# Decoder layer on one core: block products on 12 of 24 row tiles in four down products, with partial sums kept in DRAM

## The chip, the core and the metric

The kernel runs on one core of a Trainium2 chip. Its engines work side by side, each through its own list of instructions in order: PE (matrix products, and the loads of their stationary operand, PEld), DVE (two-operand arithmetic), ACT (copies, casts, activation functions), POOL (a general engine, used here for little) and SP (issues transfers). ACT and POOL issue transfers too. An instruction waits for semaphores of the others. The metric is the time of one execution in microseconds (us) on the device, less is better; it is given as the median of several runs, and one more execution was profiled.

## What is computed

A decoder layer on 256 tokens of width 2048, all in float32: an FFN, a mixer (attention beside a recurrent group) and a second FFN, each added to its scaled input and normalised. The change lies in the two FFNs alone:

```python
def swiglu(x, w_gate, w_up, w_down):
    return (jax.nn.silu(x @ w_gate) * (x @ w_up)) @ w_down
...
        x = layer_norm(alpha * x + 0.5 * swiglu(x, ffn1_w_gate[l], ffn1_w_up[l], ffn1_w_down[l]),
                       ln1_g[l], ln1_b[l])
        p = x @ w_in[l]
...
        mix = jnp.concatenate([o_attn, o_rwkv], axis=-1) @ w_out[l]
        x = layer_norm(alpha * x + mix, ln2_g[l], ln2_b[l])
        x = layer_norm(alpha * x + 0.5 * swiglu(x, ffn2_w_gate[l], ffn2_w_up[l], ffn2_w_down[l]),
                       ln3_g[l], ln3_b[l])
```

The gate and up weights are 2048 x 5632, the down weights 5632 x 2048; alpha is the fourth root of 2.

## The kernel before

**Split operands.** Every float32 operand of a large product is cut into a high part (rounded to the matrix engine's faster float format) and a low part (the rest). A product of two tiles is three matmuls: high x high, high x low of the weight, low x high (`product`, lines 151 to 153). Activations are cut once; weights are cut on the way in: a raw tile of two row tiles (128 x 1024 elements) is loaded by SP (`load`, L131), ACT casts its high part `wh` (L141), DVE subtracts for its low part `wl` (L144). The pair (`wh`, `wl`) lies in one of seven buffer pairs, used in turn (`halves`).

**Tiling.** 256 tokens are two token tiles (t = 0, 1) of 128. Weights go by row tiles of 128 rows and column blocks of 512. A matmul has 128 x 128 activations as the stationary and 128 x 512 weights as the moving operand. The 44 column blocks of the hidden width are done in two halves: 24 row tiles (six blocks of four) and then 20. For each half, gate and up are computed block by block, the hidden activations are transposed and cut into tiles `hh` (`up_done`), and then the down product adds the half's part to the layer's 2048 outputs.

**Block products.** `two_blocks` computes two column blocks at once, for both token tiles. Of the row tiles, the first eight are taken as a 2 x 2 block matrix (two groups of four row tiles by two column blocks), and the activations likewise (two token tiles by two groups of four). Their product is done in seven block products in place of eight (Winograd's form of Strassen's method): the products use sums and differences of the raw weights (`minus`, L222, DVE, in place, 128 x 2048 elements) and of the activations (`combinations`, four sums `s` that are computed, then cut into two parts each, L379 and L383). Each of the seven is `seven(...)`: two weight pairs, 12 matmuls. Partial results move between PSUM banks by ACT copies (L235, L242, L248) and DVE additions (L251, L255). The remaining row tiles go the plain way: `later` makes a list of steps of two row tiles for one column block (one weight pair, 12 matmuls for both token tiles), and `late(n)` runs n of them between the block products. The steps of the second column block are left in the list for the next call. Raw tiles of block products are four row tiles each in four buffers (`r4`), those of plain steps two row tiles in three buffers (`raw`).

**Down products.** A half calls `two_blocks` twice, for columns 0 to 1023 and 1024 to 2047. `down_done` takes each finished 128 x 512 sum: in the first half it adds alpha times the residual (loaded into `rc` by a transfer on ACT's queue, L477, which a one-column POOL copy at L476 holds back until there is use for it) and writes into the SBUF tile `y` (L478); in the second half it adds the sum to `y` and starts the normalisation (L316 on). `y0` and `y1`, 128 x 2048 each, hold these partial sums from the first half's down products to the end of the FFN. `y0` is the scratch tile of `combinations` before.

**Order.** The program is written in the order of the code; a scheduler with a cost model then puts each engine's instructions in an order by readiness and priority, which is fixed when the program is compiled. `issue_after` adds an order by hand. A tile with a tag gets its memory when the last user of the tag's former tile is done.

## Time and profile before

| | |
|---|---|
| median of 3 runs | 1919.73 us (1919.19 to 1925.22) |
| the profiled execution, its own time | 1918.89 us |
| its span, first to last instruction | 1917.1 us |
| granted PE clock, mean | 0.996 |
| FFN1 | about 0 to 680 us; its first half's down products about 252 to 377 us |
| mixer | about 680 to 1205 us |
| FFN2 | about 1206 us to the end; its first half's down products about 1456 to 1581 us |
| moved from and to HBM | 368.29 MB read, 11.80 MB written, 198 GB/s |

How to read it: a group row has the source line, engine, operation and tiles (out<-in), its count, busy time in us and the mean ns of one instruction, and after the second bar the idle time of that engine just before them with what ended it. A row of the order in time has the start, the length in us, engine, line and operation, and in brackets the idle time before it. In a row of waits, who waited for whom is followed by the total in us, how many times, and the longest. Lines (L144) are those of the code above. Matmuls are pipelined: the 390 ns of one overlap those of the next.

### The profile page before, as it was taken

What the parts mean: (1) busy time and instruction counts of PE and PEld (TensorE: products, weight loads), DVE (VectorE), ACT (ScalarE), POOL (GpSimd) and SP (SyncE); (2) the same over time, 40 slices, a digit from 0 to 9 for tenths busy, and PEclk for the clock granted to TensorE, in tenths of its full rate; (3) what the DMA queues carried; (4) which work ended last, traced back from release to release, by engine and by line L of the source; (5) the groups of instructions that cost most, each with busy time, mean ns of one, the idle gap of its engine ahead of it and who ended that gap; (6) DMA issues with size and microseconds to landing.
All of it is one profiled execution on the core that took longest, in us unless ns stands there. A gap on an engine that the chain in (4) does not pass through costs nothing. (4 is left out here: it accounts for less than half of the span.)

```text
span 1917.1 us, 24935 instructions
## 1 busy us (share of the span) xinstructions
PE 1881.4 (98%) x9335; PEld 1547.7 (81%) x9335; DVE 1623.1 (85%) x1834; ACT 1093.9 (57%) x1376; POOL 74.9 (4%) x110
## 2 busy tenths in 40 slices
PE   8999999999999999999999999999999999999997
PEld 7888888888888878887778877788888888888886
DVE  8999987789999976776678886999999778999986
ACT  6656664566666536645565543566666545666651
POOL 0000101100000000000000000000000110000000
PEclk9999999999999999999999999999999999999999
DMA  9766676765667456555445645775566676566744
GB/s 312 246 201 217 185 239 220 233 212 200 216 213 228 143 172 201 167 159 160 139 132 146 188 135 165 257 255 191 197 214 227 208 245 211 198 205 212 223 159 134
DMA packets 207322, 381.73 MB, mean 199 GB/s; under 512 B 23531, under 2 KB 25649, under 8 KB 206945
## 3 DMA queue, kind: packets, MB, share of 16 engines
q1 hardware_dynamic: 182928, 350.53, 55.7%
q0 software_dynamic: 6832, 15.32, 3.0%
q10 hardware_dynamic: 17440, 14.29, 2.6%
q8 instruction: 73, 1.20, 0.3%
q14 instruction: 49, 0.39, 0.1%
HBM read 368.29 MB, written 11.80 MB: 198 GB/s over the span
## 5 line engine op out<-in xcount | busy, mean ns | idle before, releaser
L141 ACT CAST wh<-raw 128x1024 fp32r<-128x1024 f32 (+2 forms) x833 | 852.6, 1047 | 596.6 <-PE acc L153 365.9
L144 DVE TENSOR_TENSOR wl<-raw,wh 128x1024 fp32r<-128x1024 f32 (+2 forms) x833 | 983.3, 1213 | 207.7 <-ACT wh L141 203.7
L152 PE MATMUL acc<-wl,xh 128*128 128x512 f32 (+1 forms) x1552 | 604.6, 391 | 4.0 <-DVE wl L144 4.0
L153 PE MATMUL acc<-wh,xl 128*128 128x512 f32 (+1 forms) x1552 | 603.2, 390 | 0.5 <-DVE xl L90 0.4
L151 PE MATMUL acc<-wh,xh 128*128 128x512 f32 (+1 forms) x1552 | 597.8, 393 | 5.9 <-ACT xh L89 4.6
L151 PEld LDWEIGHTS acc<-wh,xh 128*128 128x128 f32 x1552 | 291.7, 188 | 69.3 <-ACT xh L89 6.2
L152 PEld LDWEIGHTS acc<-wl,xh 128*128 128x128 f32 x1552 | 292.0, 188 | 63.6 <-DVE wl L144 5.4
L153 PEld LDWEIGHTS acc<-wh,xl 128*128 128x128 f32 x1552 | 292.0, 188 | 61.8 <-DVE xl L90 2.0
L222 DVE TENSOR_TENSOR raw<-raw,raw 128x2048 f32<-128x2048 f32 x112 | 255.8, 2284 | 1.0 <-DMA raw<-in_ffn_w_gate_dram 0.5
L152 PE MATMUL acc<-wl,hh 128*128 128x512 f32 x544 | 212.0, 390 | 0.0
L153 PE MATMUL acc<-wh,hh 128*128 128x512 f32 x544 | 211.4, 389 | 0.0
L151 PE MATMUL acc<-wh,hh 128*128 128x512 f32 x544 | 210.9, 390 | 0.0
L151 PE MATMUL acc<-wh,s 128*128 128x512 f32 x448 | 174.9, 390 | 1.0 <-ACT acc L248 1.0
L153 PE MATMUL acc<-wh,s 128*128 128x512 f32 x448 | 174.6, 390 | 0.0
L152 PE MATMUL acc<-wl,s 128*128 128x512 f32 x448 | 174.4, 389 | 0.0
L151 PEld LDWEIGHTS acc<-wh,hh 128*128 128x128 f32 x544 | 102.1, 188 | 21.7 <-ACT wh L141 0.4
L152 PEld LDWEIGHTS acc<-wl,hh 128*128 128x128 f32 x544 | 102.2, 188 | 21.1
L153 PEld LDWEIGHTS acc<-wh,hh 128*128 128x128 f32 x544 | 102.1, 188 | 20.9
L151 PEld LDWEIGHTS acc<-wh,s 128*128 128x128 f32 x448 | 84.1, 188 | 19.0 <-ACT acc L248 1.5
L153 PEld LDWEIGHTS acc<-wh,s 128*128 128x128 f32 x448 | 84.1, 188 | 17.5
L152 PEld LDWEIGHTS acc<-wl,s 128*128 128x128 f32 x448 | 84.1, 188 | 17.4
L235 ACT COPY acc<-acc 128x512 f32<-128x512 f32 x28 | 16.0, 571 | 51.5 <-PE acc L153 47.7
(264 smaller groups left out, 1100.0 us busy)
## 6 DMA issues: line engine op xcount, KB each, us to landing
raw<-in_ffn_w_up_dram SPq DMA_DIRECT2D x176, 512.0 KB, 5.3
raw<-in_ffn_w_down_dram SPq DMA_DIRECT2D x176, 512.0 KB, 5.4
raw<-in_ffn_w_gate_dram SPq DMA_DIRECT2D x175, 512.0 KB, 4.5
raw<-in_w_in_dram SPq DMA_DIRECT2D x96, 512.0 KB, 3.7
raw<-in_w_out_dram SPq DMA_DIRECT2D x32, 512.0 KB, 4.1
sd<-s POOLq DMA_DIRECT2D x16, 256.0 KB, 4.1
s<-sd POOLq DMA_DIRECT2D x16, 256.0 KB, 5.1
xs<-y ACTq DMA_DIRECT2D x16, 256.0 KB, 3.0
```

Of the source, the lines that this page charges most:

```text
L141: SC.copy(out=wh[:, c, :w], in_=raw[:, c, :w])
L144: self.cut = V.tensor_tensor(out=wl[:, c, :w], in0=raw[:, c, :w], in1=wh[:, c, :w].bitcast(F32), op=ALU.subtract).ins
L151: T.matmul(a, hi, wh[:, j, :w], start=first and j == 0, stop=False, skip_group_check=True)
L152: T.matmul(a, hi, wl[:, j, :w], start=False, stop=False, skip_group_check=True)
L153: i = T.matmul(a, lo, wh[:, j, :w], start=False, stop=last and j == 1, skip_group_check=True)
L222: V.tensor_tensor(out=out, in0=x, in1=y, op=ALU.subtract)
L235: SC.copy(out=u, in_=a)
```

## The change

In the two down calls of each FFN's first half, `extra` is set. There the block products cover 12 row tiles, not 8: each of the seven has two row tiles more (`whole` and `comb` map j = 4, 5 to them), so three weight pairs and 18 matmuls, and the plain steps cover 12 row tiles, not 16. `own` loads a second raw tile of two row tiles for each of the four blocks, and `minus` runs on both. The activations of the third group of four row tiles (hidden block 2) get their own sums, at half width, by `half_tiles`. For room, the seventh pair's two buffers and `y0`'s place hold the additional raw tiles, so the calls use six weight pairs; `y1`'s place holds the additional activation sums. The partial sums therefore leave SBUF: `down_done` writes its result in place in `rc` and stores it to DRAM tiles `ys` on ACT's queue, and `y` is loaded back by POOL's queue in the second call of the second half (j = 1).

```diff
@@ -203,9 +203,9 @@
                 for t in range(2):
                     use(t)
 
-        def two_blocks(self, cols, ks, x, comb, done, strict=False):
+        def two_blocks(self, cols, ks, x, comb, done, strict=False, extra=None):
             assert not self.pend
-            self.buffers(NW["ffn"], LAG["ffn"])
+            self.buffers(NW["ffn"] - (extra is not None), LAG["ffn"])
             (s0, c0), (s1, c1) = cols
             if self.roles is None:
                 self.roles = [(self.rot + i) % NACC["ffn"] for i in range(6)]
@@ -215,34 +215,46 @@
             a, z, u, w = (self.bank(i) for i in self.roles[:4])
             row = ks[0][0]
 
-            def own(src, k, c):
-                return self.load(src, row + k, c, n=4)
+            done_rows = 8
+            if extra is not None:
+                done_rows = 12
+                more = dict(zip(("11", "12", "22", "21"), extra()))
+
+            def own(src, k, c, name):
+                r = [self.load(src, row + k, c, n=4)]
+                if extra is not None:
+                    t = more[name]
+                    self.loaded = nc.sync.dma_start(out=t, in_=src[(row + 8 + k // 2) * P:(row + 10 + k // 2) * P, c:c + NB].rearrange("(k p) n -> p k n", p=P)).ins
+                    r.append(t)
+                return r
 
             def minus(out, x, y):
-                V.tensor_tensor(out=out, in0=x, in1=y, op=ALU.subtract)
+                for o, a, b in zip(out, x, y):
+                    V.tensor_tensor(out=o, in0=a, in1=b, op=ALU.subtract)
 
             def seven(acc, lhs, raw, first=False, last=False):
-                for i in range(2):
-                    self.product(acc, lambda j: lhs(2 * i + j), *self.halves(raw[:, 2 * i:2 * i + 2]), first and i == 0, last and i == 1)
+                parts = [raw[0][:, 0:2], raw[0][:, 2:4]] + raw[1:]
+                for i, r in enumerate(parts):
+                    self.product(acc, lambda j: lhs(2 * i + j), *self.halves(r), first and i == 0, last and i + 1 == len(parts))
 
             def whole(t, k):
-                return lambda j: x(t, k + j)
+                return lambda j: x(t, k + j if j < 4 else 4 + k // 2 + j)
 
             n = len(self.tail) // 4
             with tc.issue_after(self.loaded) if strict else ExitStack():
-                r11 = own(s0, 0, c0)
+                r11 = own(s0, 0, c0, "11")
             seven(a, whole(0, 0), r11, True)
             SC.copy(out=u, in_=a)
             self.late(n)
             with tc.issue_after(self.loaded) if strict else ExitStack():
-                r12 = own(s1, 0, c1)
+                r12 = own(s1, 0, c1, "12")
             minus(r11, r12, r11)
             seven(z, comb(0), r11, True, True)
             s5 = self.pool.tile([P, NB], F32, tag="s5", name=nm("s5"))
             SC.copy(out=s5, in_=z)
             self.late(n)
             with tc.issue_after(self.loaded) if strict else ExitStack():
-                r22 = own(s1, 4, c1)
+                r22 = own(s1, 4, c1, "22")
             minus(r11, r22, r11)
             seven(u, comb(1), r11)
             SC.copy(out=w, in_=u)
@@ -254,9 +266,9 @@
             v = self.bank(self.roles[4])
             V.tensor_tensor(out=v, in0=w, in1=s5, op=ALU.add)
             with tc.issue_after(self.loaded) if strict else ExitStack():
-                r21 = own(s0, 4, c0)
+                r21 = own(s0, 4, c0, "21")
             seven(a, whole(0, 4), r21)
-            self.later(s0, c0, ks[8:], x, (a, w), lambda t, acc: done(0, t, acc), False)
+            self.later(s0, c0, ks[done_rows:], x, (a, w), lambda t, acc: done(0, t, acc), False)
             n = len(self.tail) // 4
             self.late(n)
             seven(u, comb(3), r22)
@@ -264,7 +276,7 @@
             minus(r11, r21, r11)
             seven(w, whole(1, 4), r11)
             self.late(len(self.tail))
-            self.later(s1, c1, ks[8:], x, (u, v), lambda t, acc: done(1, t, acc), False)
+            self.later(s1, c1, ks[done_rows:], x, (u, v), lambda t, acc: done(1, t, acc), False)
 
         def flush(self, lag=0):
             uses = []
@@ -373,13 +385,13 @@
 
         S = {}
 
-        def combinations(x, tmp, after=None):
+        def combinations(x, tmp, after=None, own=None):
             def add(out, x, y, op=ALU.add):
                 x, y = (a if a.dtype == F32 else a.bitcast(F32) for a in (x, y))
                 V.tensor_tensor(out=out, in0=x, in1=y, op=op)
 
             def cut(x, i):
-                hi, lo = s_tiles(i)
+                hi, lo = (own or s_tiles)(i)
                 SC.copy(out=hi, in_=x)
                 add(lo, x, hi, ALU.subtract)
 
@@ -403,7 +415,7 @@
             return S[i]
 
         def comb(i):
-            return lambda j: (S[i][0][:, j, :], S[i][1][:, j, :])
+            return lambda j: tuple(s[:, j, :] for s in S[i]) if j < 4 else tuple(s[:, j - 4, :] for s in S[4 + i])
 
         def y_parts():
             t = fp.tile([P, 4, 4, P], F32, tag="y0", name=nm("xs"))
@@ -411,6 +423,24 @@
 
         def x_parts():
             return [xp.tile([P, 4, P], F32, tag=f"{t}0{q}", name=nm("xs")) for q in range(2) for t in ("xh", "xl")]
+
+        def half_tiles(x):
+            u = fp.tile([P, 8, 2, P], F32R, tag="y1", name=nm("s"))
+            t = fp.tile([P, 4, 2, P], F32, tag="y0", name=nm("xs"))
+
+            def own(i):
+                S[4 + i] = [u[:, 2 * i], u[:, 2 * i + 1]]
+                return S[4 + i]
+
+            combinations({(a, q): [h[:, 2 * q:2 * q + 2] for h in x[(a, 2)]] for a in range(2) for q in range(2)},
+                         [t[:, i] for i in range(4)], None, own)
+
+        def more_raws():
+            r = [fp.tile([P, 2, NB], F32, tag=f"{n}6", name=nm("raw")) for n in ("wh", "wl")]
+            t = fp.tile([P, 4, NB], F32, tag="y0", name=nm("raw"))
+            return r + [t[:, 0:2], t[:, 2:4]]
+
+        ys = [dp.tile([P, D], F32, tag=f"ys{t}", name=nm("ys")) for t in range(2)]
 
         for half, nj in enumerate((6, 5)):
             hT = {}
@@ -457,6 +487,10 @@
                         for i in range(4):
                             for k, t in enumerate(s_tiles(i)):
                                 nc.gpsimd.dma_start(out=t, in_=sd[i, k])
+                    if half == 1 and j == 1:
+                        y.extend(fp.tile([P, D], F32, tag=f"y{t}", name=nm("y")) for t in range(2))
+                        for t in range(2):
+                            nc.gpsimd.dma_start(out=y[t], in_=ys[t])
                     stream.two_blocks(((wg, c0), (wu, c0)), KX, x_lhs, comb, lambda i, tt, acc, f=(gate_done, up): f[i](tt, acc), j0 + j == 1)
 
             def h_lhs(tt, k, hT=hT):
@@ -465,7 +499,7 @@
 
             combinations(hT, (y_parts, x_parts)[half]())
             if half == 0:
-                y.extend(fp.tile([P, D], F32, tag=f"y{t}", name=nm("y")) for t in range(2))
+                half_tiles(hT)
             if half == 0 and extra is not None:
                 extra(hT[(0, 0)][0][:, 0, 0:1].bitcast(F32))
 
@@ -475,7 +509,8 @@
                     rc = fp.tile([P, NB], F32, tag="sg", name=nm("rc"), bufs=2)
                     G.tensor_copy(out=rc[:, 0:1], in_=hT[(0, 0)][0][:, 0, 0:1].bitcast(F32))
                     nc.scalar.dma_start(out=rc, in_=res[tt][:, c])
-                    V.scalar_tensor_tensor(out=y[tt][:, c], in0=rc, scalar=ALPHA, in1=acc, op0=ALU.mult, op1=ALU.add)
+                    V.scalar_tensor_tensor(out=rc, in0=rc, scalar=ALPHA, in1=acc, op0=ALU.mult, op1=ALU.add)
+                    nc.scalar.dma_start(out=ys[tt][:, c], in_=rc)
                 else:
                     ln_stats(tt, y[tt][:, c], acc, st[tt], n)
                     if n == 3:
@@ -483,7 +518,8 @@
 
             ks = [(j0 * 4 + k, k) for k in range(nj * 4)]
             for n in (0, 2):
-                stream.two_blocks(((wd, n * NB), (wd, (n + 1) * NB)), ks, h_lhs, comb, lambda i, tt, acc, n=n, f=down_done: f(tt, acc, n + i))
+                stream.two_blocks(((wd, n * NB), (wd, (n + 1) * NB)), ks, h_lhs, comb, lambda i, tt, acc, n=n, f=down_done: f(tt, acc, n + i),
+                                  extra=more_raws if half == 0 else None)
             if half == 1:
                 gb.extend(load_gb_over_x(lg, lb))
                 stream.flush(NW["ffn"] - 1)
```

## Prediction

> **What bounds the kernel now.** I read first the page's busy times with its slices, then the chain of work that ended last, then the busy times by window around the down products of each FFN's first half (252 to 377 us in FFN1, 1456 to 1581 us in FFN2, 125 us for two calls each), and there the waits, the groups and the order in time.
>
> ```profile
> PE 1881.4 (98%) x9335; PEld 1547.7 (81%) x9335; DVE 1623.1 (85%) x1834; ACT 1093.9 (57%) x1376; POOL 74.9 (4%) x110
> PE   8999999999999999999999999999999999999997
> DVE  8999987789999976776678886999999778999986
> PE 36%; DVE 1%; issue 0%; ACT 0%; DVEq 0%
> ```
> ```profile
> 252.00:377.00 125.00, 125.00 (x558) 103.46 (x557) 100.67 (x89) 68.33 (x73) 13.73 (x16) 1.00 0.70 232
> 1456.00:1581.00 125.00, 125.00 (x557) 103.61 (x557) 99.54 (x85) 67.08 (x71) 13.09 (x16) 1.00 0.69 225
> 420.00:505.00 85.00, 85.00 (x384) 70.54 (x383) 77.91 (x66) 52.52 (x59) 0.00 (x0) 1.00 0.60 199
> ```
> The columns after the window are its length, then busy time (and instructions) of PE, weight load, DVE, ACT, POOL, then granted clock, DMA share and GB/s. PE has work in every slice and is busy for the whole of both down windows; the chain names PE and hardly anything else (the shares it can name). So time is won by taking matmuls away, as long as DVE and ACT deliver the split weights early. In gate and up (420 to 505) DVE is busy 77.91 of 85, or 92%; in the down windows 100.67 of 125, or 81%. The down products are where DVE has spare time, and that is where the change adds work.
>
> ```profile
> 239.40 0.39 PE L151 MATMUL acc<-wh,xh 128*128 128x512 f32 x1
> 252.09 0.39 PE L153 MATMUL acc<-wh,xl 128*128 128x512 f32 x1
> DVE wl L144 <- ACT wh L141: 23.4, 16, 5.2
> ACT wh L141 <- PE acc L153: 21.6, 16, 2.8
> ACT wh L141 <- DMA raw<-in_ffn_w_down_dram: 15.3, 9, 5.4
> ACT wh L141 <- POOL rc L476: 3.8, 1, 3.8
> ```
> The first two rows are the first and last of 57 matmuls in a row: 12.69 us over 56 steps is 0.227 us a matmul; the 390 ns of one overlap the next. The other four are waits in 252 to 377 (total, times, longest). DVE waits 23.4 us, nearly all for ACT's cast; ACT in turn waits most often for a matmul to free a weight pair: then all seven pairs are full and DVE is as far ahead as it can be. The waits for DMA and for POOL are of another kind: they don't shrink by themselves when DVE has more to do.
>
> **The change, part by part.** *Matmuls, removed.* A call multiplies 8 of its 24 row tiles in seven block products of 4 row tiles, 3 matmuls each (84), and 16 in the plain way, 4 x 3 each (192): 276. With 12 row tiles it is 7 x 6 x 3 = 126 and 12 x 12 = 144: 270. Six fewer a call, four calls: 24 x 0.227 = 5.44 us less on PE, which is the bound. The page "TensorE: Matmul & The Clock Gate" of the Trainium skill (Part 1) gives N ÷ 2.4 GHz plus about 2.5 ns, 215.7 ns for 512 columns, by which the saving would be 5.18 us; this trace's rows are 5% slower.
>
> *Casts and combinations of weights, added.* Pairs split per call: 7 x 2 + 16 = 30 before, 7 x 3 + 12 = 33 after. Each of the four subtractions of raw weights gets a second one of half the size.
>
> ```profile
> L144 DVE TENSOR_TENSOR wl<-raw,wh 128x1024 fp32r<-128x1024 f32 x63 | 74.6, 1219 | 23.9 <-ACT wh L141 23.4
> L222 DVE TENSOR_TENSOR raw<-raw,raw 128x2048 f32<-128x2048 f32 x9 | 20.6, 2284 | 0.0
> L141 ACT CAST wh<-raw 128x1024 fp32r<-128x1024 f32 x61 | 62.0, 1051 | 51.0 <-PE acc L153 21.6 <-DMA raw<-in_ffn_w_down_dram 15.3 <-DVE raw L222 6.2
> L952 DVE TENSOR_TENSOR BK<-BK,vv 128x1024 f32<-128x1024 f32 x2 | 2.4, 1217 | 0.0
> L947 DVE TENSOR_TENSOR BK<-BK 128x1024 f32<-128x1024 f32 x2 | 2.5, 1225 | 9.0 <-ACT BK L945 9.0
> L903 DVE TENSOR_TENSOR St<-St,PC 128x256 f32<-128x256 f32 x4 | 1.6, 411 | 0.0
> L1026 DVE SCALAR_TENSOR_TENSOR s<-s,rr 128x256 f32<-128x256 f32 x8 | 3.8, 478 | 0.0
> L799 ACT COPY BT<-sm 128x256 f32<-128x256 f32 x16 | 5.0, 380 | 7.0 <-PE sm L797 7.0
> ```
> Per FFN DVE gets 6 more splits at 1.22 us (7.3) and 8 subtractions of 128x1024 at 1.22 (1.217 to 1.225; 9.8). ACT gets 6 casts at 1.05 (6.3). *The third block of the activations*: 8 additions and 4 residues of 128x256 on DVE, 0.41 us each by the nearest tensor row (0.48 by the other), 4.9 us (to 5.7), and 4 casts on ACT at 0.38, 1.5 us. Together 22.0 us on DVE and 7.8 on ACT per FFN. The listed durations overlap their neighbours: the splits' busy time is 74.6 for 63, or 1.18 each, so about 26 x 0.04 = 1 us comes off: 21 us.
>
> DVE's stage then holds 100.7 + 21 = 121.7 us, against PE's 125 - 2.7 = 122.3. ACT holds 76 and stays cover. So nothing is left of DVE's 24 us of idle time: what hides the added work is idle time that was lost in waiting for full buffers, and the lead that DVE has.
>
> *Where it pinches.* The half-size activation block needs the scratch tile of the full-size combinations, so it can't be done early; it falls in front of the first down call, in which the first combined product needs it.
>
> ```profile
> 251.16 2.35 DVE L144 TENSOR_TENSOR wl<-raw,wh 128x1024 fp32r<-128x1024 f32 x2
> 257.91 0.39 PE L151 MATMUL acc<-wh,s 128*128 128x512 f32 x1
> 1454.08 3.49 DVE L144 TENSOR_TENSOR wl<-raw,wh 128x1024 fp32r<-128x1024 f32 x3
> 1461.70 0.39 PE L151 MATMUL acc<-wh,s 128*128 128x512 f32 x1
> 294.54 4.63 DVE L144 TENSOR_TENSOR wl<-raw,wh 128x1024 fp32r<-128x1024 f32 x4 [4.38 <-ACT wh L141]
> 314.69 2.36 DVE L144 TENSOR_TENSOR wl<-raw,wh 128x1024 fp32r<-128x1024 f32 x2 [2.04 <-ACT wh L141]
> 357.01 4.63 DVE L144 TENSOR_TENSOR wl<-raw,wh 128x1024 fp32r<-128x1024 f32 x4 [5.21 <-ACT wh L141]
> ```
> In FFN1 the first split in front of that product ends at 251.16 + 1.2 = 252.4 and PE takes it at 257.91: a lead of 5.5 us. In FFN2 it is 1461.70 - 1455.3 = 6.4 us. Put in front now: 4.9 (activation block), 1.2 (third pair of the first product), 1.2 (second subtraction), 7.3 us; PE gets 6 matmuls more to do first, 1.4 us. Short by 7.3 - 1.4 - 5.5 = 0.4 us in FFN1, covered by 0.5 us in FFN2. The next product repeats it: 3 splits, one plain split, 2.28 + 1.22 of subtraction make 8.4 us on DVE against 30 matmuls, 6.8 us: short by another 1.6. I take PE stalls of 0.4 + 1.6 = 2.0 us in FFN1 and 1.6 - 0.5 = 1.1 in FFN2. After that a call gives back: the plain steps at its end (four splits, 4.9 us, for 48 matmuls, 10.9 us) refill the buffers. Bounds: none, where the schedule spreads the block over gaps; and all 7.3 us a FFN where the lead is already spent.
>
> *Six weight pairs, not seven.* 276 matmuls for 30 pairs are 9.2 matmuls, 2.1 us, a pair: the lead shrinks by that much, but the waits of 4.4 and 5.2 us (294.54, 357.01) are still within the 12.5 us of six pairs. Nothing by itself; a rival with the rest. *Loads.* The queue of SP issues 24 weight loads of 512 KB a call, as before (8 + 16; now 8 + 4 + 12), so bytes don't change. Two of the new raw tiles take the seventh pair's place and two the old place of the partial sums, which their last users free during the call before.
>
> *Partial results through DRAM.*
> ```profile
> xs<-y ACTq DMA_DIRECT2D x16, 256.0 KB, 3.0
> lnb<-in_ln_b_dram POOLq DMA_DIRECT2D x1, 1024.0 KB, 8.3
> rc<-xs ACTq DMA_DIRECT2D x16, 256.0 KB, 5.4
> ```
> Per FFN 8 stores of 256 KB on ACT's queue (3.0 us to land, as the like store) and 2 loads of 1 MB on POOL's queue (8.3). The loads are issued in the second call of the second half, whole calls before the sums are used; POOL has nothing behind them that PE waits for. That is 4 MB a FFN; 232 GB/s take a DMA share of 70%, so the other 30% is some 100 GB/s, 40 us for 4 MB that are spread over the 125 us and the calls behind: hidden. The stores do one thing more: a store waits on ACT for the addition, and casts queue behind it. The scratch tile comes free 3 us later, so the next prefetch of the residual waits, and ACT behind it; the nearest row is the 3.8 us wait for POOL above, once in this window, which PE does not feel (2.04 us of DVE idle at 314.69). I take nothing for it; its ends are 0 and 3.8 us for each of 4 pairs of sums a FFN, 30 us if no cover were left. A gain beyond the 5.44 has no place to come from, PE having no gap in these windows.
>
> *Sum.* -5.4 + 2.0 + 1.1 = -2.3 us on the profiled execution of 1918.9 us (span 1917.1): 1916.6. The median of the runs, 1919.7, is 0.8 above it, so 1917.4. About 0.3% (5.8 us) is what a measurement of this kernel can tell from no change, and the whole saving is 0.28%.
>
> **The rivals.** *All of it is hidden.* If the stalls stay under 1 us, the saving shows whole: 1919.7 - 5.4 = 1914.3. For it: ACT waits 21.6 us for full buffers in this window, so DVE could do that much more at once. Against it: 21 us is added, at its densest where the lead is 5.5.
>
> *DVE becomes the bound.* The three long pauses quoted above (4.38, 2.04 and 5.21, 11.6 us) stay, since loads and POOL cause them, on top of 121.7 us of work: 133.3 against PE's 122.3, 11 short a FFN. If the lead of 5.5 covers half of it, 5.5 us a FFN come on top of my stalls: 1917.4 + 11 = 1928; with no cover 1917.4 + 22 = 1939. It decides from 2.7 us of stall a FFN on. For it: 92% DVE load in the calls that follow, which give the lead back slowly (7 us in 85). Against it: those waits fall where DVE had run ahead, and loads are asked for as DVE frees raw tiles, so a slower DVE meets them later. The Trainium skill's "Trace Analysis" (Identifying the Most-Contended Engine) does not count matmul busy time but that of the weight loads: here 103.46 of 125 for these, 100.67 for DVE, so by that rule DVE takes the lead as the most contended engine after the change, and the time would go this way; the trace's even spacing of 0.227 us speaks for PE so far.
>
> *A stall halves the clock.*
> ```profile
> 1206.00:1213.00 7.00, 6.29 (x20) 4.56 (x20) 7.00 (x10) 2.60 (x4) 0.00 (x0) 0.52 0.72 226
> ```
> Where PE had pauses between the mixer and FFN2, the clock fell to 0.52 for 7 us. If one stall of the down stage were as long, some 3.4 us would come on top each time: 2 stalls, 1917.4 + 2 x 3.4 = 1924. Against it: my stalls are of 1 to 2 us, and the clock is 1.00 in both windows. (The clock gate's page, Part 1, names an idle window of about 3.4 us; this rival needs one stall that long, and no run here shows the limit.)
>
> **How the numbers follow.** Partly hidden, stalls of 1 to 8 us in all: 0.47, with its own range 1915 to 1922. All hidden: 0.25. DVE as the bound, 9 us and up: 0.18. Halved clock: 0.07. Something else, mostly an order of instructions that this change upsets elsewhere: 0.03. The time is that of the first, 1917.4. From 1913.6 (all hidden, less 0.7 of scatter among runs) to 1929 leaves out less than 2 in 10. Faster by over 0.3% needs under 1914.0: a third of the all-hidden case, 0.08. Slower by over 0.3%, above 1925.5: 0.15 of the DVE case, 0.04 of the clock's and 0.02 of the rest, 0.21. Within: 0.71.
>
> **What would show it.** Right: 24 fewer matmuls; PE still full in the down windows but for two short waits near the first combined product of each FFN, for a split or a cast; DVE at 97% or more there; ACT's waits for free weight pairs gone in these stages and back in the second half's gate and up. Wrong: DVE busy clearly below that while PE waits (then it is loads or ACT's queue: look for casts waiting for POOL or for the addition); waits of PE through both calls (DVE is the bound); a clock below 1.00 there.

## The result and the profile after

| | before | changed |
|---|---|---|
| median, measured side by side | 1922.1 us (4 runs) | 1935.17 us (1933.85 to 1935.93, 4 runs) |
| ratio, 95% interval | | 1.0075 [1.0059, 1.0091] |
| profiled execution, span | 1917.1 us | 1933.8 us |
| matmuls | 9335 | 9311 |

The change makes the kernel 0.75% slower by the ratio, 13 us by the medians. 1917.4 us was forecast, and 1929.0 was the upper end.

Page of the changed kernel: busy times, and the slices of PE and of its granted clock.

```profile
PE 1884.8 (97%) x9311; PEld 1546.6 (80%) x9311; DVE 1661.3 (86%) x1886; ACT 1109.0 (57%) x1396; POOL 81.0 (4%) x114
PE   8999989999999999999999999999998999999997
PEclk9999989999999999999999999999999999999999
```

The 24 matmuls are gone, and yet PE is busy for longer: part of the matmuls ran at a lower clock. The 8 in the sixth slice of both rows (242 to 290 us) is where FFN1's down products begin.

Busy time by window of the changed kernel (columns as in the prediction): the two down stages, a stretch of gate and up, and the 11 us inside the first stage where PE loses most.

```profile
252.00:377.00 125.00, 118.78 (x508) 96.25 (x507) 107.55 (x102) 71.41 (x78) 14.90 (x14) 0.96 0.67 227
1463.00:1588.00 125.00, 117.96 (x502) 95.22 (x501) 106.61 (x97) 71.40 (x77) 14.30 (x14) 0.97 0.65 216
420.00:505.00 85.00, 85.00 (x385) 70.54 (x384) 78.16 (x66) 53.03 (x59) 0.00 (x0) 1.00 0.68 233
279.00:290.00 11.00, 7.91 (x20) 5.55 (x21) 8.82 (x10) 4.91 (x6) 1.93 (x2) 0.53 0.51 175
```

PE was busy for 125.00 of 125 in both windows before. Now it misses 6.2 and 7.0 us, and the clock is below 1.00. Gate and up are as they were. In the same 125 us PE gets through 508 matmuls in place of 558.

Order in time on PE of the changed kernel, the rows with a pause in FFN1 and in FFN2 (start, length, in brackets the pause and what ended it):

```profile
277.34 0.66 PE L459 MATMUL tr<-ident,sg 128*128 128x128 f32 x4 [1.92 <-DVE sg L456]
281.16 0.79 PE L151 MATMUL acc<-wh,s 128*128 128x512 f32 x1 [3.16 <-ACT wh L141]
284.95 0.63 PE L153 MATMUL acc<-wh,s 128*128 128x512 f32 x1
286.24 0.79 PE L151 MATMUL acc<-wh,s 128*128 128x512 f32 x1 [0.66 <-ACT acc L260]
289.88 0.40 PE L151 MATMUL acc<-wh,s 128*128 128x512 f32 x1
...
1543.57 0.73 PE L151 MATMUL acc<-wh,hh 128*128 128x512 f32 x2 [1.34 <-ACT wh L141]
1546.14 0.63 PE L153 MATMUL acc<-wh,hh 128*128 128x512 f32 x1
```

The pauses stand at block products on sums (`s`) and at the transposes beside them in the first call of FFN1 (277 to 286 us) and of FFN2, and once at a plain product (`hh`) in the second call of FFN2 (1543.57). Behind them a matmul takes 0.63 us, not 0.39: that is the halved clock. It lasts for 10.2 us from 279.2, for 3.4 us from 1494.3 and for 3.4 us from 1545.5.

A ledger over the matmuls of the two down stages (240 to 390 us and 1440 to 1600 us) adds up how far the distance from one matmul's start to the next exceeds what it is without a pause (0.227 us for two matmuls of 512 columns): before 0.4 and 0.2 us, changed 11.4 and 12.7. That is 23.5 us more lost. 5.4 us were saved by fewer matmuls, so 18 us are left. A second count gives the same: the time from one matmul ahead of a stage to one behind it, taken at the same two matmuls in both profiles, is 8.3 us longer in FFN1 and 9.7 in FFN2, 18.0 together. The spans differ by 16.7 only, because the code outside, which is the same, ran 1.0 us slower at the start and 2.4 us faster between the stages in this execution. Of the 23.5 us, 13.3 are the pauses themselves (6.2 and 7.0 in the windows above) and some 7 are matmuls at half clock (17.1 us, of which 2.9 are pauses, at half the pace); the rest was not resolved further.

What PE waited for in the first calls is DVE, mostly through ACT. Order in time on DVE of the changed kernel around FFN1's first pauses:

```profile
266.12 4.63 DVE L144 TENSOR_TENSOR wl<-raw,wh 128x1024 fp32r<-128x1024 f32 x4
270.66 0.42 DVE L391 TENSOR_TENSOR s<-xs,s 128x256 fp32r<-128x256 f32 x1
270.99 1.22 DVE L144 TENSOR_TENSOR wl<-raw,wh 128x1024 fp32r<-128x1024 f32 x1
272.13 2.29 DVE L233 TENSOR_TENSOR raw<-raw,raw 128x2048 f32<-128x2048 f32 x1
274.33 2.36 DVE L144 TENSOR_TENSOR wl<-raw,wh 128x1024 fp32r<-128x1024 f32 x2
276.60 0.69 DVE L456 SCALAR_TENSOR_TENSOR sg<-sg,acc 128x512 f32<-128x512 f32 x1
277.20 2.36 DVE L233 TENSOR_TENSOR raw<-raw,raw 128x1024 f32<-128x1024 f32 x2
279.47 0.69 DVE L456 SCALAR_TENSOR_TENSOR sg<-sg,acc 128x512 f32<-128x512 f32 x1
```

No row has a bracket: DVE runs without a break. The last step of gate and up (L456) stands behind a full-size subtraction and two splits, so PE's transposes (L459) come late. Behind it stand two of the new half-size subtractions (277.20 to 279.56), and the cast that PE waits for next starts at 280.06; ACT had stood for 1.37 us behind POOL until then. Over the whole window DVE is idle for 17 us, but not here.

DVE's work also comes to PE by a longer way, through POOL and then ACT. Rows of DVE, POOL, ACT and PE of the changed kernel in front of the longest pause of FFN2:

```profile
1488.97 3.50 DVE L144 TENSOR_TENSOR wl<-raw,wh 128x1024 fp32r<-128x1024 f32 x3
1489.30 3.33 POOL L510 COPY rc<-hh 128x1 f32<-128x1 f32 x2 [228.24 <-PE tr L459]
1492.94 0.58 ACT L469 CAST hh<-tr 128x512 fp32r<-128x512 f32 x1 [3.15 <-POOL rc L510]
1494.07 0.60 PE L151 MATMUL acc<-wh,s 128*128 128x512 f32 x1 [2.41 <-ACT acc L260]
```

POOL's one-column copies, which hold back the residual's prefetch, end just behind DVE's run of splits (1492.63 after 1492.47). ACT has the prefetch ahead of its other work and stands for 3.15 us; its copy of a partial sum (L260) starts at 1493.44, and PE has waited 2.41 us for it. So the question was: which part of the added DVE work, at which place, makes the pauses?

### The profile page after: what moved, and what is told of

Its sections match the earlier page's. It is cut to its first block, busy times and chain, and to the rows that moved or that the text cites. A ratio compares the mean times of both kernels' runs of the same rounds, so it can differ in the third digit from the quotient of the medians.

```text
span 1933.8 us, 25000 instructions
## 1 busy us (share of the span) xinstructions
PE 1884.8 (97%) x9311; PEld 1546.6 (80%) x9311; DVE 1661.3 (86%) x1886; ACT 1109.0 (57%) x1396; POOL 81.0 (4%) x114
## 5 line engine op out<-in xcount | busy, mean ns | idle before, releaser
L141 ACT CAST wh<-raw 128x1024 fp32r<-128x1024 f32 (+1 forms) x845 | 865.1, 1047 | 602.0 <-PE acc L153 394.8
L144 DVE TENSOR_TENSOR wl<-raw,wh 128x1024 fp32r<-128x1024 f32 (+1 forms) x845 | 997.5, 1216 | 189.3 <-ACT wh L141 184.3
L233 DVE TENSOR_TENSOR raw<-raw,raw 128x2048 f32<-128x2048 f32 (+1 forms) x128 | 275.5, 2155 | 1.9 <-DMA raw<-in_ffn_w_up_dram 1.1
L151 PE MATMUL acc<-wh,s 128*128 128x512 f32 x480 | 190.0, 396 | 8.9 <-ACT wh L141 4.9
L152 PE MATMUL acc<-wl,hh 128*128 128x512 f32 x504 | 197.1, 391 | 0.0
L153 PE MATMUL acc<-wh,hh 128*128 128x512 f32 x504 | 196.8, 391 | 0.0
L151 PE MATMUL acc<-wh,hh 128*128 128x512 f32 x504 | 192.7, 391 | 1.3 <-ACT wh L141 1.3
L152 PE MATMUL acc<-wl,s 128*128 128x512 f32 x480 | 188.9, 394 | 0.7 <-DVE wl L144 0.7
L153 PE MATMUL acc<-wh,s 128*128 128x512 f32 x480 | 188.6, 393 | 0.0
L151 PEld LDWEIGHTS acc<-wh,s 128*128 128x128 f32 x480 | 91.2, 190 | 31.2 <-ACT wh L141 6.9
L151 PEld LDWEIGHTS acc<-wh,hh 128*128 128x128 f32 x504 | 94.6, 188 | 21.9 <-ACT wh L141 2.5
L152 PEld LDWEIGHTS acc<-wl,hh 128*128 128x128 f32 x504 | 94.9, 188 | 19.9
L153 PEld LDWEIGHTS acc<-wh,hh 128*128 128x128 f32 x504 | 95.0, 189 | 19.7
L153 PEld LDWEIGHTS acc<-wh,s 128*128 128x128 f32 x480 | 91.2, 190 | 19.2
```

The lines of the kernel that those rows point to most:

```text
L141: SC.copy(out=wh[:, c, :w], in_=raw[:, c, :w])
L144: self.cut = V.tensor_tensor(out=wl[:, c, :w], in0=raw[:, c, :w], in1=wh[:, c, :w].bitcast(F32), op=ALU.subtract).ins
L151: T.matmul(a, hi, wh[:, j, :w], start=first and j == 0, stop=False, skip_group_check=True)
L152: T.matmul(a, hi, wl[:, j, :w], start=False, stop=False, skip_group_check=True)
L153: i = T.matmul(a, lo, wh[:, j, :w], start=False, stop=last and j == 1, skip_group_check=True)
L233: V.tensor_tensor(out=o, in0=a, in1=b, op=ALU.subtract)
```

## The experiments

All ratios are against the kernel before, measured beside it. Line numbers in rows are those of the kernel that was run.

**Partial sums through DRAM alone** (kernel before, plus this):

```diff
-V.scalar_tensor_tensor(out=y[tt][:, c], in0=rc, ...)
+V.scalar_tensor_tensor(out=rc, in0=rc, ...)
+nc.scalar.dma_start(out=ys[tt][:, c], in_=rc)
...
```

(Not shown: `y` is loaded back on POOL's queue, as in the changed kernel.)

> The kernel before with the partial sums alone sent through DRAM (12 row tiles, six pairs and the additional tiles left out; full computation). Theory A (the sums of the third activation block come late, in front of the first down call, and PE starves there): nothing here but the stores' wait on ACT, which DVE's spare time covers: within 2 us of before, no new clock drop. Theory C (a store, its landing, the POOL copy and ACT's prefetch hold up the casts): ACT still waits 7 to 8 us once per FFN, PE pauses over 1 us near the second down call, 3 to 8 us slower than before.

1922.64 us, ratio 1.0000 [0.9990, 1.0011]. Window of this kernel:

```profile
252.00:377.00 125.00, 125.00 (x557) 103.42 (x557) 99.73 (x88) 67.11 (x72) 11.14 (x15) 1.00 0.70 240
```

PE stays full. The stores and loads alone cost nothing that can be measured.

**Six weight pairs alone** (kernel before, `NW["ffn"] - 1` in the first half's down calls):

> The kernel before with six weight pairs, not seven, in the first half's down calls; nothing else. Theories A and C: no difference, under 1 us, PE without a pause there. A rival, that the shorter lead by itself starves PE: pauses in the down windows and over 3 us slower.

1922.65 us, 1.0004 [0.9992, 1.0017]. Nothing.

**Without the half-width activation sums** (changed kernel; the third row-tile group's sums are left out and slices of the full-width sums stand in their place):

```diff
-                half_tiles(hT)
+                for i in range(4):
+                    S[4 + i] = [s[:, 0:2] for s in S[i]]
```

> The changed kernel without the half-width sums of the third activation block: the additional products take slices of the sums that are there, so the output differs; 12 DVE and 4 ACT instructions fewer per FFN, and the additional raw tiles no longer wait for that scratch tile. Theory A: the pauses of PE near the first combined products (6.0 us in FFN1, 5.5 in FFN2) and the clock drops of 10.2 and 3.4 us there go; 10 to 13 us faster than the changed kernel, about 1924. Theory B (DVE is short in the whole stage, whatever the place): only the 4.5 us a FFN of this work come back, less than 7 us in all, and pauses remain. Theory C: the drop of the clock at the second down call of FFN2 stays in either case.

1932.99 us, 1.0057 [1.0040, 1.0074]. **Half-width sums ahead of the full-width ones** (changed kernel, all work done; `half_tiles(hT)` moved in front of `combinations(hT, ...)`):

> The changed kernel with the half-width sums written ahead of the full-width ones, so that they use the scratch tile first and can run in gaps of gate and up; all work is done. Theory A: like the run without these sums, about 1924, pauses at the first combined product gone or under 2 us. Theory B: no gain, within 3 us of the changed kernel, since DVE has as much to do.

1933.09 us, 1.0056 [1.0039, 1.0073]. Order in time on PE, pauses of the first (280.22) and second call of the kernel with the sums moved:

```profile
280.22 0.50 PE L151 MATMUL acc<-wh,s 128*128 128x512 f32 x1 [0.66 <-ACT acc L260]
329.12 0.50 PE L151 MATMUL acc<-wh,s 128*128 128x512 f32 x1 [1.42 <-ACT wh L141]
331.01 0.73 PE L151 MATMUL acc<-wh,hh 128*128 128x512 f32 x2 [1.39 <-ACT wh L141]
1541.80 0.73 PE L151 MATMUL acc<-wh,hh 128*128 128x512 f32 x2 [2.41 <-ACT wh L141]
1544.17 0.79 PE L151 MATMUL acc<-wh,s 128*128 128x512 f32 x1 [1.64 <-ACT wh L141]
```

The first call's pauses shrink to 0.7 us and less in FFN1 and to 1.0 us and less in FFN2, but new ones open in the second call, with a halved clock in both FFNs. My first theory, that the sums came too late and pushed one pile in front of the first call, fell: PE arrives earlier and meets the next pile. In this second pile DVE is not the last link: it stood idle itself for 1.62 us before 327.20, waiting for ACT's cast, and ACT had stood for 5.76 us with the prefetch ahead of it.

**Without the second subtractions** (changed kernel; the 16 subtractions of the additional raw tiles are left out):

```diff
-                for o, a, b in zip(out, x, y):
+                for o, a, b in list(zip(out, x, y))[:1]:
```

> The changed kernel without the second, half-width subtraction of raw weights (16 DVE instructions of 1.2 us fewer; left out, so the output differs). Theory A is dropped: the runs without the half sums and with them early gained only 2 us, and a pause near the second down call stayed. Theory B (the stage as a whole has too much DVE work in front of the combined products, so each of the two calls of a stage starves): 20 us of DVE work less, most of the pauses gone, 8 to 14 us faster than the changed kernel. Theory C (ACT held by the prefetch of the residual): the pauses at the second call stay, 2 to 5 us faster.

1916.99 us, 0.9981 [0.9971, 0.9990]. Window of this kernel:

```profile
252.00:377.00 125.00, 124.97 (x556) 103.09 (x555) 107.15 (x102) 75.58 (x82) 9.85 (x14) 1.00 0.71 240
```

PE is full, the clock 1.00, and the saving shows; ACT still waits for POOL's copies, in FFN2's window up to 4.4 us at a time, and PE has no pause from it. DVE is as busy in this window as in the changed kernel (107.15 against 107.55), since it gets through more of the call. **Without either** (both edits above, both pieces of work left out):

> The changed kernel without the half-width sums and without the second subtractions (left out, so the output differs); the three more splits a call stay, and ACT's queue is as in the changed kernel. Theory B: no pauses, the saving shows, 1914 to 1917. Theory C: the pause at the second call stays, 1919 to 1924.

1916.75 us, 0.9980 [0.9968, 0.9991]: the half-width sums cost nothing once the second subtractions are gone.

**The second subtraction on its own tile** (changed kernel; it has the same length and place but reads only the tile that it writes, so it waits for no other load; its result is another):

> The changed kernel with the second subtractions kept as DVE work of the same length in the same place, but each reading its own tile alone (it subtracts the tile from itself, so the output differs): the wait for the other block's additional raw tile is gone. Theory B (DVE time in front of the combined products): as slow as the changed kernel, 1930 to 1936. Rival D (the wait for a second raw tile, which comes late since its place is freed late): near the run without the second subtractions, 1917 to 1921.

1933.61 us, 1.0071 [1.0059, 1.0083], as slow as the changed kernel. It is DVE's time at that place, not the wait for a second tile.

**The same DVE time at the end of the call** (second subtractions left out; in each call eight 128x512 subtractions without use are put among the plain steps behind the last block product):

```diff
-            self.late(len(self.tail))
+            for i in range(len(self.tail)):
+                self.late(1)
+                for _ in range(2 if extra is not None and i < 4 else 0):
+                    V.tensor_tensor(out=s5, in0=s5, in1=s5, op=ALU.subtract)
```

> The changed kernel without the second subtractions, but with as much DVE time (8 subtractions of 128x512 on a scratch tile, 5.4 us a call against 4.9) set among the plain steps at the end of each call (the output differs). Theory B in the form that place counts: DVE is ahead there, so within 3 us of the run without them, about 1917 to 1920. Theory B in the form that the stage's total counts: as slow as the changed kernel, 1930 to 1936.

1923.21 us, 1.0010 [0.9999, 1.0021]. Its window, and the group of added instructions there:

```profile
252.00:377.00 125.00, 122.08 (x529) 99.87 (x528) 111.02 (x112) 74.12 (x80) 10.38 (x14) 0.97 0.70 234
L281 DVE TENSOR_TENSOR s<-s 128x512 f32<-128x512 f32 x16 | 11.0, 685 | 0.0
```

11.0 us of DVE work a FFN at the end of the calls cost 0.29% against the kernel without it (1.0010 - 0.9981); 9.8 us in front of the products cost 0.94% (1.0075 - 0.9981). Place counts for more than amount. It is not free even there: a pause of 1.53 us at 325 us, in the second call of FFN1, halved the clock. In front of it ACT stood for 3.32 us behind POOL's copy, and DVE for 1.61 us behind ACT.

**The transfers of the partial sums on POOL's queue**, in place of ACT's (changed kernel), and **the same with the half-width sums first**:

> The changed kernel with the stores of the partial sums and the residual's prefetch on POOL's queue, not on ACT's; the work is the same. Theory C: the pauses near 330 us and 1541 us and the clock drop there go, 3 to 6 us faster than the changed kernel; the pause at the first combined product stays. Theory B: ACT waits less, but DVE is what is short, so under 2 us.

> The changed kernel with both: half-width sums ahead of the full-width ones, and stores and prefetch on POOL's queue; all work is done. If the two causes are separate, pauses at the first and the second call both go and the 5.4 us of matmuls show: 1916 to 1922. Theory B alone: still 1930.

1940.19 us, 1.0101 [1.0086, 1.0115], and 1930.85 us, 1.0046 [1.0032, 1.0061]. What they were to remove is this. Orders in time of the changed kernel on ACT (first two rows), POOL and DVE:

```profile
332.08 0.82 ACTq L511 DMA_DIRECT2D rc<-in_x_dram  x2
333.03 2.95 ACT L141 CAST wh<-raw 128x1024 fp32r<-128x1024 f32 x3 [7.67 <-POOL rc L510]
326.11 6.06 POOL L510 COPY rc<-hh 128x1 f32<-128x1 f32 x2 [41.90 <-DMA ys<-rc]
328.58 3.43 DVE L233 TENSOR_TENSOR raw<-raw,raw 128x2048 f32<-128x2048 f32 x2
334.11 3.50 DVE L144 TENSOR_TENSOR wl<-raw,wh 128x1024 fp32r<-128x1024 f32 x3 [2.10 <-ACT wh L141]
```

A store lands, POOL's copies of one column run (6.06 us for two, to 332.17, while DVE runs without a break to 332.01), and ACT, which has the next transfer ahead of its casts, stands for 7.67 us. DVE then stands for 2.10 us behind ACT. With the partial sums through DRAM alone, ACT stood for 3.58 us at this place. Pauses on PE in the second call, kernel with sums first and POOL's queue:

```profile
327.43 0.51 PE L151 MATMUL acc<-wh,s 128*128 128x512 f32 x1 [0.59 <-ACT wh L141]
329.32 0.72 PE L151 MATMUL acc<-wh,hh 128*128 128x512 f32 x2 [1.39 <-ACT wh L141]
```

ACT's wait for the prefetch accounts for a part: the pause of 1.39 us stays, and in front of it ACT now waits 3.46 us for DVE's subtraction. Counted at the same matmuls, the two stages are 11.9 us longer than before with the sums first, and 8.4 with the POOL queue too. With the sums in their old place the POOL queue made it worse: a new pause of 4.20 us at 1573 us, in front of which DVE stood for 6.13 us for the residual.

**The second subtractions on POOL** (changed kernel):

```diff
+                for e, o, a, b in zip((V, G), out, x, y):
+                    e.tensor_tensor(out=o, in0=a, in1=b, op=ALU.subtract)
```

> The changed kernel with the second subtractions on POOL, not on DVE; all work is done. If DVE's time is all that counts and POOL disturbs nothing: like the run without them, 1917 to 1920. If POOL takes several us for each, with DVE and POOL slowing each other as the one-column POOL copies of 3 to 6 us suggest: pauses remain, 1928 to 1940.

1944.15 us, 1.0127 [1.0108, 1.0146], the slowest. Groups in 252 to 377 us of this kernel:

```profile
L233 POOL TENSOR_TENSOR raw<-raw,raw 128x1024 f32<-128x1024 f32 x8 | 26.5, 3312 | 68.1 <-DVE wl L144 52.1 <-DMA raw<-in_ffn_w_down_dram 15.9
L144 DVE TENSOR_TENSOR wl<-raw,wh 128x1024 fp32r<-128x1024 f32 x61 | 83.8, 1407 | 18.1 <-ACT wh L141 17.5
```

A subtraction takes 3.31 us on POOL, and DVE's splits beside it slow from 1.22 to 1.41 us in the mean. The work costs DVE time on POOL too.

**Sums first, and the plain steps spread** (changed kernel, all work done). In the second call six plain steps of the first are left over; `len(self.tail) // 4` runs them 1, 1, 1 and the last three together, where before the change eight ran 2, 2, 2, 2:

```diff
-            n = len(self.tail) // 4
+            n = -(-len(self.tail) // 4)
```

> The changed kernel with the half-width sums ahead of the full-width ones, and the six plain steps that are left from the first call spread 2, 2, 2 over the first three products of the second call, not 1, 1, 1, 3; all work is done. If place counts, the pause near 330 us and 1542 us and its clock drop go, the small ones at the first call stay: 1922 to 1927. If the total counts: 1930 and up.

1921.59 us, 1.0000 [0.9989, 1.0012]. **The spread alone** (sums where the change has them):

> The changed kernel with the plain steps of the second call spread 2, 2, 2 instead of 1, 1, 1, 3, and the half-width sums where the change has them. Theory: the pauses of the second call (1.34 us at 1543 in the changed kernel, and those at 325 to 330 of the runs that healed the first call only) go or stay under 0.7 us, the first call's at 277 to 286 and 1483 to 1494 stay with their clock drop, so it lies between the changed kernel and the run with both edits: 1924 to 1931, ratio 1.001 to 1.005, and the clock at 0.5 shows near 280 us but not near 330 or 1545. Rival (the order of the half-width sums was what healed the run with both edits, the spread did nothing): ratio as in the run with the half-width sums first alone or worse, 1.006 to 1.008, with the pause at 1543 still there. Rival (the spread alone did it all): ratio 1.000 and no pauses at 277 to 286.

1937.42 us, 1.0079 [1.0063, 1.0096]. Window of the kernel with both edits, then a pause of the one with the spread alone:

```profile
252.00:377.00 125.00, 123.25 (x543) 100.54 (x543) 112.51 (x100) 73.04 (x78) 11.72 (x14) 1.00 0.70 239
```
```profile
279.96 0.79 PE L151 MATMUL acc<-wh,s 128*128 128x512 f32 x1 [3.16 <-ACT wh L141]
```

With both edits no pause is over 0.66 us in these windows and the clock stays at 1.00. The ledger's loss is 5.3 us where the changed kernel has 24.0 and the kernel before 0.6, so the extra 4.8 us eat most of the 5.4 saved; counted at the same matmuls the two stages take as long as before (0.0 us). The second edit also spreads the six steps left over in the second call of the second half, but no pause over 0.6 us stood in the second halves (380 to 680 us and 1595 to 1870 us) of the changed kernel or of this one. The spread alone removes the second call's pause, as expected, and leaves the first call's; its price was foreseen too low (1.001 to 1.005), for the clock was then at half for 10.2 us in both FFNs, where the changed kernel lost 3.4 us at that place in FFN2. Each edit alone leaves one of two piles, and one pile with its halved clock is enough for 0.6 to 0.8%.

**12 row tiles in the second call only** (both edits above, `extra` for n = 2 alone), and **that with six pairs in both calls**:

> The edit of the run with the half-width sums first and the plain steps spread, and besides that block products on 12 row tiles in the second down call of each first half alone; the first call keeps 8. Theory of a local pile of DVE work in front of the combined products: the second call has plain steps of a longer queue from the first call between its products (two and more after each), so its four extra subtractions fit; the first call is what it was before. No PE pause over 1 us in either call, clock 1.00, and 12 matmuls less at 0.227 us = 2.7 us: 1919 to 1920 where the kernel before takes 1922, ratio 0.9985 to 0.999. Rival (any subtraction on the second half of a pair, wherever it is, costs its own 1.22 us on the way to the products): 4 of them in each FFN, 9.8 us, against 2.7 us: 1929, ratio 1.004. Rival (the gain is eaten by what feeds the block, half-width sums and stores): ratio 1.000 or above without pauses at combined products.

> The run with block products on 12 row tiles in the second call alone, but with six weight pairs in both calls of the first half, not seven in the first and six in the second. In the run with seven then six, SyncE's queue held an extra weight load of the second call (L227) 2.1 us for the matmuls that still read the seventh pair, whose place the load takes; it landed at 311.2 us, ACT and DVE waited for it (DVE idle 2.7 us ahead of 312.3), the subtractions then came in one run, and PE paused 1.14 us at 321.7 (1.32 us at 1530.4). Theory (the late place made that pile): with the place free from the start the loads go out earlier, no pause over 0.7 us in the second call, the first call as before, and the saving of 12 matmuls x 0.227 = 2.7 us is left: ratio 0.9975 to 0.9995, some 1918 to 1920 where the kernel before takes 1921 to 1922. Rival (the four extra subtractions of a call themselves make the pause, early loads or not): pauses over 1 us stay near 321 and 1530 and the ratio is 1.000 to 1.002. Rival (six pairs in the first call make a pause there): gaps over 0.7 us between 270 and 290.

1924.37 us, 1.0011 [1.0000, 1.0021], and 1923.59 us, 1.0011 [1.0001, 1.0021]. SP's wait and PE's pauses in the first of them; then the second one's windows:

```profile
SPq L227 <- PE acc L153: 2.1, 1, 2.1
321.66 0.50 PE L152 MATMUL acc<-wl,s 128*128 128x512 f32 x1 [1.14 <-DVE wl L144]
1530.42 0.50 PE L152 MATMUL acc<-wl,s 128*128 128x512 f32 x1 [1.32 <-DVE wl L144]
```
```profile
252.00:377.00 125.00, 124.62 (x554) 102.84 (x553) 107.03 (x95) 73.18 (x78) 10.43 (x14) 1.00 0.73 244
1463.00:1588.00 125.00, 125.00 (x556) 103.39 (x556) 104.75 (x90) 67.97 (x71) 13.36 (x16) 1.00 0.70 229
```

With seven pairs in the first call, an extra load of the second waited for the seventh pair's place, and a pause came of it, against what I expected; with six pairs in both, the pauses in the second call are gone, as the theory has it. The time is not: 1918 to 1920 was expected. Counted at the same matmuls, its two stages are 1.3 us shorter than before, of 2.7 saved. But its profiled execution is the fastest of its twelve, which range from 1919.6 to 1926.1 us, as those of before beside it do from 1918.2 to 1926.5. The stretch between the two stages, whose code is the same in every kernel here, took from 2.4 us less to 5.0 us more in the other profiles than in that of before. A clock at half for 3.4 us near 713 us, between FFN1 and the mixer, stands in this profile and not in that of before, but also in the one with six pairs alone (712.0) and without the second subtractions (709.9). So whether the 1.3 us are a gain can't be told from these times. None of the versions that do all of the work beats the kernel before; sums first with spread steps (1.0000) beats the change.

## Why the prediction was wrong

**The step that failed is "Where it pinches": "I take PE stalls of 0.4 + 1.6 = 2.0 us in FFN1 and 1.6 - 0.5 = 1.1 in FFN2. After that a call gives back".** The term of 3.1 us came out at 23.5, so the two stages took 18.0 us longer and not 2.3 us less. Three things in it were wrong.

- *It counted two products of one call.* The pile of subtractions recurs in the second call, and the same change thins out what lies between the products there: six plain steps are left over in place of eight, so one runs behind each product, not two. With the pile in front of the first call relieved (sums first) the pauses stood at 329 to 331 and 1541 to 1544 us; with the steps spread they went. The plain steps that were to give back were in the call, but behind the last product.
- *It set work against lead as if DVE did the pile in PE's order, and as if the pile reached PE through the splits alone.* The last gate and up step (L456) stood behind other work, and two half-size subtractions ahead of what PE needed (277.34 and 281.16 in the rows above). At 1494.07 the pile came through POOL's copies and ACT's queue, which the prediction took as nothing. How the 23.5 us divide between the two ways is open.
- *It priced a pause at its length.* Behind most of the longer ones the clock was at half, 17.1 us in all.

Taking DVE's stage total (121.7 against PE's 122.3) as the thing to compare misled in the same way: the measured window has DVE at 107.55 of 125 with PE waiting, and the kernel with the same DVE time at the calls' end has 111.02 and is 0.6% faster than the change.

**Right:** the matmul term (24 fewer; 0.9981 where the subtractions are left out, 3.6 us of 5.4 in the times, 5.0 us in the spans of 1917.1 and 1912.1, the second of which is the fastest of ten; the two stages alone are 5.0 us shorter there); DVE's durations (128x1024 subtraction 1.22 us, 128x256 sum 0.42); six pairs, nothing; partial sums through DRAM, nothing (1.0000).

**A bound too low:** the wait of ACT behind the stores was given 3.8 us at the most for each pair of sums; in the changed kernel it was 7.67 and 7.91 us in the second calls. With the sums first and the transfers on POOL's queue two of the second call's pauses shrank by 0.8 to 1.0 us (1.42 to 0.59, 2.41 to 1.39), yet the ratio moved from 1.0056 to 1.0046 only, with intervals that overlap. What this wait is worth by itself is not settled.

**Loads** were taken as nothing. In the changed kernel SP's queue stood for a half-width sum once in FFN1 (3.4 us) and twice in FFN2 (10.4 and 2.2 us); with the sums first most of the first call's pauses went, so order and load place together were worth something in that call, which the runs don't separate.

**The rivals.** "DVE becomes the bound" had the time in its span (1928 to 1939), and its condition, 2.7 us of stall a FFN, was met (6.2 and 7.0 us of pauses). Its reason was half right: not the stage's total, but the density in front of the products; that the time lay in its span was in part luck, since its sum had no clock in it. By the rule of "Perfetto Trace Analysis" in the Trainium skill (Identifying the Most-Contended Engine) DVE leads after the change, 107.55 against 96.25 of weight loads, and the outcome agrees; but the run with the work at the end has DVE ahead too (111.02 against 99.87) at 1.0010, so the ranking by busy time doesn't give the price here. "A stall halves the clock" had 0.07 and came true on top; "this rival needs one stall that long" was wrong, see below. Of "what would show it", the signs for wrong came: waits of PE in both calls, casts waiting for POOL, a clock below 1.00, and DVE at 86% of the window while PE waited. By the prediction the last sign points at loads or ACT's queue; but without the second subtractions the same loads and the same queue made no pause. ACT's waits for free pairs did not go (22.5 us in 23 times, before 21.6 in 16).

## What to carry to other kernels

Where a bound engine is fed by another through a few buffers, compare the feeder's work with the lead product by product, in the order of its queue, and not stage by stage: 9.8 us of work a FFN cost 0.94% in front of the products and about the same amount 0.29% behind them. When a change takes steps away, look at the integer divisions that spread the rest between the heavy parts. Follow the feeder's work through the other engines too: here it also held POOL, and through it ACT's queue. And price a pause of PE with the clock that it may take along, not by its length alone.

## What was not expected of the hardware

**Pauses of 1.3 us were followed by a halved clock, sometimes.** Windows around the same pause of 2.17 us at 989.9 us (mixer, untouched code), first in the kernel with 12 row tiles in the second call only, then in the same with six pairs in both calls:

```profile
989.00:994.00 5.00, 4.10 (x12) 3.24 (x13) 4.98 (x10) 1.13 (x4) 0.47 (x1) 0.66 0.41 109
```
```profile
989.00:994.00 5.00, 4.16 (x19) 3.46 (x20) 4.92 (x10) 1.95 (x5) 0.52 (x1) 1.00 0.42 112
```

Clock 0.66 in one, 1.00 in the other. The traces show what differs. In each of them, the stretches at half clock start and end on a grid of slots of 3.413 us, whose phase is another in each trace: in the changed kernel the starts at 279.18, 1494.33 and 1545.53 us are 356 and 15 slots apart. In the first of the two traces, the pause fell into one slot of the grid, in which PE was busy for 0.36 of the time, and the next slot was at half clock. In the second it fell across two, with 0.47 and 0.89, and the clock stayed. Over all 17 traces of this case, each of the 55 slots at full clock in which PE was busy for less than 0.43 was followed by a slot at half clock, and none of the 9248 with 0.64 or more; of the 83 between, 30 were. In the changed kernel 1.34 us at 1543.57, with 0.21 us behind it, lay in one slot (0.54) and were followed by 3.4 us at half; in the run with 12 row tiles in the second call only, 1.32 us at 1530.42 fell across two (0.78 and 0.67) and were not.

"TensorE: Matmul & The Clock Gate" of the Trainium skill (Part 1) says that the clock drops after an idle window of about 3.4 us, and that the window runs freely, so that its phase differs from run to run. The grid and its phase agree with that; but PE need not be idle for the whole of a window, as the busy shares of 0.36 and 0.54 in front of a drop show.

**POOL is slow beside DVE.** A one-column copy takes 0.18 us where DVE does no split or subtraction beside it (307.64 us in the kernel before). Of the copies that hold back the prefetch, 158 in all traces took longer than 0.25 us, and every one ended within 0.06 us of the end of a split or a subtraction on DVE. The two copies at 326.11 us in the changed kernel took 6.06 us, while DVE ran without a break, and the 128x1024 subtraction took 3.31 us on POOL against 1.22 on DVE. "Perfetto Trace Analysis" of the Trainium skill (Optimizing Scalar/DVE Operations) says that the two share a read port of SBUF and that moving work between them may not help; the ratio of 1.0127 agrees.
